# Weight tiles of the down projections: the low part made by an accumulating DMA in place of a VectorE subtraction

## The chip, the cores and the metric

The kernel runs on one core of a Trainium2 chip. The metric is device time in microseconds (us), from one launch to its end. The kernel before took 1015.24 us in the median of two runs (1014.68 and 1015.81).

## What is computed

The reference is a two-layer decoder trunk for 256 tokens of width 1024, in float32. Each layer is a feed-forward block, a token mixer with cross attention beside it, and a second feed-forward block:

```python
D_FF = 256 * ((8 * D_MODEL // 3 + 255) // 256)      # 2816

def swiglu(x, w_in, w_out):
    gate, up = jnp.split(x @ w_in, 2, axis=-1)
    return (jax.nn.silu(gate) * up) @ w_out
...
    for i in range(DEPTH):
        x = x + 0.5 * swiglu(rms_norm(x, ffn1_norm_g[i]), ffn1_w_in[i], ffn1_w_out[i])
...
        x = x + 0.5 * swiglu(rms_norm(x, ffn2_norm_g[i]), ffn2_w_in[i], ffn2_w_out[i])
```

The change concerns `@ w_out`, the down projection (2816 to 1024) of the four feed-forward blocks.

## The kernel before, in words

Activations are held transposed, 128 features on the partitions and 256 tokens along the row. Products are made on TensorE in a reduced float format (`F32R`), three for one: each operand is split into a high part (the value rounded to that format) and a low part (the value less its high part), and `mm3` (L226 to L230) issues high x high, high x low and low x high into one accumulator. The weights are split as they arrive, tile by tile, and each is used once.

A weight tile has 128 partitions x 4 chunks x 256 columns, 512 KB (2 chunks, 256 KB, for the last tile of each six in a down projection); a chunk of a partition is a run of 1 KB. `wtile` (L218) takes a raw buffer `wr` (5 of them, pool `wrp`), loads it by a DMA on SP's queue, and calls `split` (L208): ScalarE writes the high part `wh` by a copy (L213), and VectorE writes the low part `wl`, raw less high (L214). `wh` and `wl` have 8 buffers each. So at most 13 tiles can be under way ahead of TensorE: 8 split, and 5 raw.

Four feed-forward blocks run one after the other, with the two mixers between them (`program`, L1003). In `ffn` (L536) the up projection takes 44 tiles in eleven groups, then the down projection takes four column groups (`c2`) of 256 outputs; for each it walks the six tiles of `KG` (20 chunks in five tiles, then 2) and both halves `m` of the columns. At the end of each group VectorE scales the sum and adds it to the residual, and `Norm.put` prepares the next norm. The last group of the last block is written otherwise: it takes all six tiles first and then walks them twice (L552). 

TensorE and SP run in the order in which the program is written. The other engines' order is set by a scheduler, and each engine's queue is worked off in order. POOL (GpSimd) does little: a few small loads at the start and the powers of some norms (L253, L313, L406).

Of the kernel before, what the change touches and what calls it, by code (L numbers as in the profile page):

```python
# [10 lines left out]
F32 = mybir.dt.float32  # L11
F32R = mybir.dt.float32r
BF16 = mybir.dt.bfloat16
I32 = mybir.dt.int32
AF = mybir.ActivationFunctionType
ALU = mybir.AluOpType
# [3 lines left out]
P = 128  # L20
# [78 lines left out]
def tile_trunk(ctx: ExitStack, tc: tile.TileContext, a, out):  # L99
    nc = tc.nc  # L100
    seq = [0]

    def mk(pool, shape, dt, tag):
        seq[0] += 1
        return pool.tile(shape, dt, tag=tag, name=f"{tag}_{seq[0]}")

    def pool(name, bufs, **kw):
        return ctx.enter_context(tc.tile_pool(name=name, bufs=bufs, **kw))
# [11 lines left out]
    wrp = pool("wrp", 5)  # L120
    whp = pool("whp", 8)
    wlp = pool("wlp", 8)
# [10 lines left out]
    def act(*args, **kw):  # L133
        ins = nc.scalar.activation(*args, **kw)  # L134
        if args[2] not in (AF.Copy, AF.Square):
            tabled[0] = ins
# [6 lines left out]
    def unit(dt):  # L143
        return mk(up, [P, 2, T], dt, "u")

    def tmp():
        return mk(tp, [P, 2, T], F32, "t")
# [4 lines left out]
    def mo():  # L152
        return mk(pb8, [P, 512], F32, "bank")

    def halves(ps):
        return ps.rearrange("p (h t) -> p h t", h=2)
# [49 lines left out]
    last = [None]  # L206

    def split(src, shape):  # L208
        hi = mk(whp, shape, F32R, "wh")
        lo = mk(wlp, shape, F32R, "wl")  # L210
        n = shape[1] // pieces[0]
        for i in range(pieces[0]):
            last[0] = nc.scalar.copy(hi[:, i * n:(i + 1) * n], src[:, i * n:(i + 1) * n])  # L213
            tt(out=lo[:, i * n:(i + 1) * n], in0=src[:, i * n:(i + 1) * n],  # L214
               in1=hi[:, i * n:(i + 1) * n].bitcast(F32), op=ALU.subtract)
        return hi, lo

    def wtile(src, nk, ncol=256):  # L218
        raw = mk(wrp, [P, nk, ncol], F32, "wr")
        nc.sync.dma_start(raw, src)  # L220
        return split(raw, [P, nk, ncol])

    def wcols(w, c0, kh):
        return wtile(w.rearrange("(k p) f -> p k f", p=P)[:, kh * 4:(kh + 1) * 4, c0:c0 + 256], 4)

    def mm3(ps, wh, wl, xh, xl, start, stop):  # L226
        nc.tensor.matmul(ps, wh, xh, start=start, stop=False, skip_group_check=True)  # L227
        nc.tensor.matmul(ps, wh, xl, start=False, stop=False, skip_group_check=True)  # L228
        nc.tensor.matmul(ps, wl, xh, start=False, stop=stop, skip_group_check=True)  # L229
        wv.now += 0.328  # L230
# [24 lines left out]
    def pair(x):  # L255
        return x.unsqueeze(1).to_broadcast([P, 2, T])
# [170 lines left out]
    def memory():  # L427
# [8 lines left out]
        for c2 in range(4):  # L436
            nc.sync.dma_start(memT[c2], a["memT"][:, 2 * c2:2 * c2 + 2])
            hi, lo = unit(F32R), unit(F32R)
            for m in range(2):
                split_gain(memT[c2][:, m], g(G_MEM + 2 * c2 + m), hi[:, m], lo[:, m])  # L440
            mh.append(hi)
            ml.append(lo)
            if c2 == 0:
                v = wkv.rearrange("(k p) f -> p k f", p=P)
                wfirst.append([wtile(v[:, k:k + 2, 0:256], 2) for k in (0, 2)])
            if c2 == 2:
                wfirst.append(wcols(wkv, 0, 1))
# [50 lines left out]
    def ffn_in(x, w_in, hh, hl, mid=None):  # L498

        def hidden(ps):  # L500
            t = tmp()
            for m in range(2):
                tt(out=t[:, m], in0=ps[m][:, :T], in1=x.rb, op=ALU.mult)  # L503
            act(t, t, AF.Silu)
            for m in range(2):
                tt(out=t[:, m], in0=t[:, m], in1=ps[m][:, T:], op=ALU.mult)  # L506
            hi, lo = unit(F32R), unit(F32R)
            split_plain(t, hi, lo)
            hh.append(hi)
            hl.append(lo)  # L510

        waiting = []
        for gi in range(11):
            ps = [mo(), mo()]
            for kh in range(2):
                for part in range(2):
                    wh, wl = wcols(w_in, part * FF + gi * 256, kh)
                    for m in range(2):
                        for k in range(4):
                            kc = kh * 4 + k  # L520
                            mm3(ps[m][:, part * T:(part + 1) * T],
                                wh[:, k, m * P:(m + 1) * P], wl[:, k, m * P:(m + 1) * P],
                                x.xh[kc // 2][:, kc % 2], x.xl[kc // 2][:, kc % 2],
                                start=kc == 0 and part == 0, stop=kc == 7)
                        yield
            waiting.append(ps)
            if gi == 0 and not x.done:
                continue
            yield x.ready
            for ps in waiting:  # L530
                hidden(ps)
            waiting.clear()
            if mid is not None and gi == 5:
                wv.spawn(mid())

    def ffn(x, w_in, w_out, nxt=None, mid=None):  # L536

        pieces[0] = 1
        hh, hl = [], []
        yield from ffn_in(x, w_in, hh, hl, mid)  # L540
        w = w_out.rearrange("(k p) f -> p k f", p=P)

        def products(ps, m, kg, wt, start):
            ms = slice(m * P, (m + 1) * P)
            for k in range(kg[1]):
                kc = kg[0] + k
                mm3(ps, wt[0][:, k, ms], wt[1][:, k, ms], hh[kc // 2][:, kc % 2], hl[kc // 2][:, kc % 2],
                    start=kc == 0 and start, stop=kc == 21)

        for c2 in range(4):  # L550
            wts = [(kg, w[:, kg[0]:kg[0] + kg[1], c2 * 256:(c2 + 1) * 256]) for kg in KG]
            if nxt is None and c2 == 3:  # L552
                wts = [(kg, wtile(src, kg[1])) for kg, src in wts]
                y = tmp()
                for m in range(2):
                    ps = mo()[:, :T]
                    for kg, wt in wts:
                        products(ps, m, kg, wt, True)
                        yield
                    tt(out=y[:, m], in0=ps, in1=x.hrb, op=ALU.mult)  # L560
                    tt(out=y[:, m], in0=y[:, m], in1=x.xT[c2][:, m], op=ALU.add)
                    nc.scalar.dma_start(out[:, 2 * c2 + m], y[:, m])
                return
            ps = mo()
            for kg, src in wts:
                wt = wtile(src, kg[1])
                for m in range(2):
                    products(ps[:, m * T:(m + 1) * T], m, kg, wt, m == 0)
                    yield
            t = tmp()  # L570
            tt(out=t, in0=halves(ps), in1=pair(x.hrb), op=ALU.mult)
            xn = unit(F32)
            tt(out=xn, in0=t, in1=x.xT[c2], op=ALU.add)
            if nxt is None:
                nc.scalar.dma_start(out[:, 2 * c2:2 * c2 + 2], xn)
            else:
                nxt.put(xn)
        wv.spawn(nxt.chain(), LAT['norm'])
# [424 lines left out]
    def program():  # L1003
        yield from memory()
        x1, x2, x3 = Norm(G_MIX, half=False, cols=True), Norm(G_F2), Norm(G_F1 + 8)
        x4, x5 = Norm(G_MIX + 8, rows=False), Norm(G_F2 + 8)
        yield from ffn(x0, a["ffn1_w_in"][0], a["ffn1_w_out"][0], x1, late_constants)
        yield from mixer_a(x1, x2)
        yield from ffn(x2, a["ffn2_w_in"][0], a["ffn2_w_out"][0], x3)
        yield from ffn(x3, a["ffn1_w_in"][1], a["ffn1_w_out"][1], x4, rope_tables)  # L1010
        yield from mixer_b(x4, x5)
        yield from ffn(x5, a["ffn2_w_in"][1], a["ffn2_w_out"][1])
# [41 lines left out]
```

## Time and profile before

| what | value |
|---|---|
| median of two runs | 1015.24 us |
| span of the profiled execution, first to last instruction | 1011.9 us |
| mean granted TensorE clock | 0.997 |
| busy: PE, DVE, ACT, POOL | 98%, 67%, 52%, 3% |
| DMA traffic | 182.71 MB, 181 GB/s over the span |
| weight tiles split | 347 pairs of L213 and L214 |

The profiled execution's own time beside its span is not listed; the median of the runs lies 3.3 us above the span. The page gives busy times, shares in 40 slices, DMA queues, and the chain of work that ended last, followed back from the last instruction. PE is TensorE's matmuls and PEld its weight loads, DVE is VectorE, ACT is ScalarE, SP is the queue that issues the weights' loads, and a queue's number in the DMA part (q1, q0) stands for SP's and POOL's issues. In a row of a group `out<-in` are the program's tiles, with the mean of one and the idle time ahead of it behind the bar. In a row of the waits stand the waiting instruction, what released it, total us, times, and the longest.

### The profile page before, as it was taken

How to read it: one execution, taken by the hardware profiler on the slowest of the kernel's cores; microseconds unless marked ns; L12 is line 12 of the kernel's file. 1: busy time of each engine (PE TensorE's matmuls, PEld its weight loads, DVE VectorE, ACT ScalarE, POOL GpSimd, SP SyncE). 2: the span in 40 equal slices, each digit the busy share in tenths (PEclk: the TensorE clock that was granted, in tenths of full speed). 3: DMA queues.
4: the chain of work that ended last, by engine and by line, in shares of the span. 5: the costliest groups of instructions: out<-in, count | busy, mean ns of one | idle time of the engine just before them, and what ended most of it. 6: DMA issues, size and time to landing. Idle time of an engine off the chain costs nothing.

```text
span 1011.9 us, 20587 instructions
## 1 busy us (share of the span) xinstructions
PE 996.4 (98%) x8560; PEld 978.2 (97%) x8560; DVE 673.3 (67%) x1116; ACT 524.0 (52%) x771; POOL 28.5 (3%) x27
## 2 busy tenths in 40 slices
PE   8899999999999999999999999999999999999998
PEld 7899999999999999999999999999987899999998
DVE  6876665668756786666568666656787768666551
ACT  7755444456566564454445444544557665454440
POOL 1100000000100000000000000000121000000000
PEclk9999999999999999999999999999999999999999
DMA  9676666667644566665666666566632247665650
GB/s 310 209 247 189 193 190 180 190 187 204 184 131 138 178 191 199 193 191 178 192 206 201 200 189 192 178 194 199 189 115 81 87 137 222 199 190 183 189 171 22
DMA packets 173205, 182.71 MB, mean 181 GB/s; under 512 B 7124, under 2 KB 168328, under 8 KB 173112
## 3 DMA queue, kind: packets, MB, share of 16 engines
q1 hardware_dynamic: 171872, 179.60, 58.3%
q10 hardware_dynamic: 1016, 1.58, 0.5%
q8 instruction: 67, 1.10, 0.5%
q0 software_dynamic: 224, 0.22, 0.2%
q14 instruction: 26, 0.21, 0.1%
HBM read 180.32 MB, written 1.05 MB: 179 GB/s over the span
## 4 chain that ended last, share of the span: by engine, by line
PE 92%; DVE 4%; ACT 1%; POOL 1%; DMA 1%; issue 0%; SPq 0%; POOLq 0%; ACTq 0%; DVEq 0%
PE bank L227 29%; PE bank L228 29%; PE bank L229 29%; PE bank L233 2%; DVE wl L214 1%; PE bank L238 1%; POOL col L406 1%; ACT u L134 1%; DMA wr<-in_mem_w_kv_dram 1%; PE bank L988 1%; DVE col L401 0%; DVE u L410 0%; DVE u L973 0%; DVE col L957 0%; ACT wh L213 0%
## 5 line engine op out<-in xcount | busy, mean ns | idle before, releaser
L214 DVE TENSOR_TENSOR wl<-wr,wh 128x1024 fp32r<-128x1024 f32 (+1 forms) x347 | 414.7, 1196 | 267.0 <-ACT wh L213 266.2
L213 ACT CAST wh<-wr 128x1024 fp32r<-128x1024 f32 (+1 forms) x347 | 356.9, 1031 | 391.8 <-PE bank L228 367.4
L227 PE MATMUL bank<-xh,wh 128*128 128x256 f32 x1544 | 427.8, 277 | 0.0
L228 PE MATMUL bank<-xl,wh 128*128 128x256 f32 x1544 | 426.4, 276 | 0.0
L229 PE MATMUL bank<-xh,wl 128*128 128x256 f32 x1544 | 426.4, 276 | 0.0
L227 PEld LDWEIGHTS bank<-xh,wh 128*128 128x128 f32 x1544 | 290.0, 188 | 0.1
L228 PEld LDWEIGHTS bank<-xl,wh 128*128 128x128 f32 x1544 | 289.8, 188 | 0.1
L229 PEld LDWEIGHTS bank<-xh,wl 128*128 128x128 f32 x1544 | 289.8, 188 | 0.0
L227 PE MATMUL bank<-u,wh 128*128 128x256 f32 x896 | 249.3, 278 | 0.0
L228 PE MATMUL bank<-u,wh 128*128 128x256 f32 x896 | 247.6, 276 | 0.0
L229 PE MATMUL bank<-u,wl 128*128 128x256 f32 x896 | 247.6, 276 | 0.0
L227 PEld LDWEIGHTS bank<-u,wh 128*128 128x128 f32 x896 | 168.2, 188 | 1.9 <-issue 1.7
L228 PEld LDWEIGHTS bank<-u,wh 128*128 128x128 f32 x896 | 168.3, 188 | 0.1
L229 PEld LDWEIGHTS bank<-u,wl 128*128 128x128 f32 x896 | 168.3, 188 | 0.0
L227 PE MATMUL bank<-wh,xh 128*128 128x256 f32 x208 | 60.3, 290 | 0.0
L228 PE MATMUL bank<-wl,xh 128*128 128x256 f32 x208 | 58.7, 282 | 0.0
L229 PE MATMUL bank<-wh,xl 128*128 128x256 f32 x208 | 58.5, 281 | 0.0
L503 DVE TENSOR_TENSOR t<-bank,rb 128x256 f32<-128x256 f32 x88 | 36.3, 420 | 6.7 <-PE bank L229 6.7
L227 PEld LDWEIGHTS bank<-wh,xh 128*128 128x128 f32 x208 | 39.8, 191 | 0.5 <-issue 0.3
L228 PEld LDWEIGHTS bank<-wl,xh 128*128 128x128 f32 x208 | 39.8, 191 | 0.1
L229 PEld LDWEIGHTS bank<-wh,xl 128*128 128x128 f32 x208 | 39.8, 191 | 0.0
L506 DVE TENSOR_TENSOR t<-t,bank 128x256 f32<-128x256 f32 x88 | 32.7, 413 | 0.0
(182 smaller groups left out, 671.0 us busy)
## 6 DMA issues: line engine op xcount, KB each, us to landing
wr<-in_ffn_w_in_dram SPq DMA_DIRECT2D x176, 512.0 KB, 4.3
wr<-in_ffn_w_out_dram SPq DMA_DIRECT2D x80, 512.0 KB, 3.7
wr<-in_a_w_in_dram SPq DMA_DIRECT2D x28, 512.0 KB, 3.7
wr<-in_b_w_in_dram SPq DMA_DIRECT2D x14, 512.0 KB, 4.6
wr<-in_a_w_out_dram SPq DMA_DIRECT2D x12, 512.0 KB, 3.4
wr<-in_b_w_out_dram SPq DMA_DIRECT2D x12, 512.0 KB, 3.4
wr<-in_ffn_w_out_dram SPq DMA_DIRECT2D x16, 256.0 KB, 2.9
wr<-in_mem_w_kv_dram SPq DMA_DIRECT2D x7, 512.0 KB, 7.8
```

What stands on the lines that cost most here:

```text
L134: ins = nc.scalar.activation(*args, **kw)
L213: last[0] = nc.scalar.copy(hi[:, i * n:(i + 1) * n], src[:, i * n:(i + 1) * n])
L214: tt(out=lo[:, i * n:(i + 1) * n], in0=src[:, i * n:(i + 1) * n], in1=hi[:, i * n:(i + 1) * n].bitcast(F32), op=ALU.subtract)
L227: nc.tensor.matmul(ps, wh, xh, start=start, stop=False, skip_group_check=True)
L228: nc.tensor.matmul(ps, wh, xl, start=False, stop=False, skip_group_check=True)
L229: nc.tensor.matmul(ps, wl, xh, start=False, stop=stop, skip_group_check=True)
L233: nc.tensor.matmul(ps, lhsT, rhs, start=start, stop=stop, skip_group_check=True)
L238: nc.tensor.transpose(ps, src, ident[:k, :k])
L406: nc.gpsimd.tensor_tensor(out=u[:, 8:8 + 2 * n], in0=u[:, 0:2 * n], in1=mhalf[:, 0:2 * n], op=ALU.pow)
L503: tt(out=t[:, m], in0=ps[m][:, :T], in1=x.rb, op=ALU.mult)
L506: tt(out=t[:, m], in0=t[:, m], in1=ps[m][:, T:], op=ALU.mult)
L988: nc.tensor.matmul(o[es[e], cs], vr[:, i, js], pTs[e][:, src], start=i == 0, stop=i == 1, skip_group_check=True)
```

## The change

A second function makes weight tiles, and the down projections call it, except the last column group of the last block: 24 tiles in each of the first three blocks and 18 in the last, 90 in all.

```diff
+    def wtile_dma(src, nk):
+
+        raw = mk(wrp, [P, nk, 256], F32, "wr")
+        hi, lo = mk(whp, [P, nk, 256], F32R, "wh"), mk(wlp, [P, nk, 256], F32R, "wl")
+        nc.sync.dma_start(raw, src)
+        act(lo, raw, AF.Copy, scale=-1.0)
+        nc.gpsimd.dma_start(lo, src, accum_op=ALU.add)
+        last[0] = nc.scalar.copy(hi, raw)
+        return hi, lo
...
             ps = mo()
             for kg, src in wts:
-                wt = wtile(src, kg[1])
+                wt = wtile_dma(src, kg[1])
                 for m in range(2):
```

ScalarE writes the negative of the rounded weights into the low tile, and a DMA issued on POOL's queue reads the same weights from DRAM once more and adds them onto it, so that the low tile holds the weight less its rounded value. The raw load on SP's queue and the copy to the high tile stay. VectorE has no part in these tiles any more. TensorE's third product of a triple, the first that reads the low tile, waits for the DMA where it waited for VectorE.

The order of TensorE's and SP's instructions is the same as before but for line numbers, which are 10 higher below the new function. On ScalarE, at the start of the first down projection, there stood before (`t` and `u` belong to the up projection's groups, `wh` and `wl` to weight tiles):

```order
L213 CAST wh_1987<-wr_1985 128x1024
L134 ACTIVATE t_1751<-t_1751 128x512
L213 CAST wh_2028<-wr_2026 128x1024
L247 CAST u_1757<-t_1751 128x512
L213 CAST wh_2058<-wr_2056 128x1024
L213 CAST wh_2088<-wr_2086 128x1024
```

And now:

```order
L213 CAST wh_1987<-wr_1985 128x1024
L134 ACTIVATE t_1751<-t_1751 128x512
L230 CAST wh_2027<-wr_2026 128x1024
L257 CAST u_1757<-t_1751 128x512
L134 ACTIVATE wl_2028<-wr_2026 128x1024
L230 CAST wh_2058<-wr_2057 128x1024
L134 ACTIVATE wl_2059<-wr_2057 128x1024
L230 CAST wh_2089<-wr_2088 128x1024
```

Each tile has a second instruction on ScalarE, behind the high part's; the up projection's instructions keep their places between them.

On POOL, from the powers of the memory's keys to those of the first mixer, there stood before (`col` are the norms' columns):

```order
L406 TENSOR_TENSOR col_418<-col_418,mhalf_116 128x4
L185 DMA u_110<-in_mask_dram 128x384
L406 TENSOR_TENSOR col_3160<-col_3160,mhalf_116 128x4
L406 TENSOR_TENSOR col_3233<-col_3233,mhalf_116 128x4
L253 TENSOR_TENSOR col_3798<-col_3809,mhalf_116 128x2
```

Now the 24 accumulating DMAs of the first block stand between them, of which these are the first three:

```order
L416 TENSOR_TENSOR col_418<-col_418,mhalf_116 128x4
L185 DMA u_110<-in_mask_dram 128x384
L229 DMA wl_2028<-in_ffn_w_out_dram 128x4x256
L229 DMA wl_2059<-in_ffn_w_out_dram 128x4x256
L229 DMA wl_2090<-in_ffn_w_out_dram 128x4x256
```

and these the last two, with the mixer's powers behind them:

```order
L229 DMA wl_2715<-in_ffn_w_out_dram 128x4x256
L229 DMA wl_2746<-in_ffn_w_out_dram 128x2x256
L416 TENSOR_TENSOR col_3184<-col_3184,mhalf_116 128x4
L416 TENSOR_TENSOR col_3257<-col_3257,mhalf_116 128x4
L263 TENSOR_TENSOR col_3822<-col_3833,mhalf_116 128x2
```

No power stands between the DMAs of one block.

## Prediction

> **What bounds the kernel now.** I read the page's shares and slices first, then the chain that ended last, then the waits, and at last the one stage that the change touches. From the page:
>
> ```profile
> span 1011.9 us, 20587 instructions
> PE 996.4 (98%) x8560; PEld 978.2 (97%) x8560; DVE 673.3 (67%) x1116; ACT 524.0 (52%) x771; POOL 28.5 (3%) x27
> PE   8899999999999999999999999999999999999998
> DMA  9676666667644566665666666566632247665650
> PE 92%; DVE 4%; ACT 1%; POOL 1%; DMA 1%; issue 0%; SPq 0%; POOLq 0%; ACTq 0%; DVEq 0%
> ```
>
> TensorE is busy in every slice and carries 92% of the chain. VectorE, which the change relieves, carries 4%. So a saving on VectorE is worth only what TensorE waits for it. All such waits on a low part, in the whole run and then in the first down projection (window 160 to 220; columns: total us, times, longest):
>
> ```profile
> PEld bank L228 <- DVE wl L214: 3.4, 2, 2.3
> PE bank L228 <- DVE wl L214: 3.0, 2, 2.1
> ...
> ACT wh L213 <- PE bank L228: 30.2, 21, 2.1
> DVE wl L214 <- ACT wh L213: 24.1, 19, 2.5
> ```
>
> The first two rows are the whole price of late low parts, and they lie elsewhere: within the down projection TensorE is not among the waiting engines. There ScalarE waits for TensorE (a place in the ring of eight), and VectorE for ScalarE. TensorE sets the pace. Its pace and the other engines' room, from the tile's rows and from three windows (us, busy of PE, PEld, DVE, ACT, POOL, clock, DMA share, GB/s):
>
> ```profile
> L227 PE MATMUL bank<-u,wh x176: 276/276/276, 160.3 to 219.8; 128*128 128x256 f32 x176
> L229 PE MATMUL bank<-u,wl x176: 276/276/276, 160.5 to 220.0; 128*128 128x256 f32 x176
> ...
> 160.00:220.00 60.00, 60.00 (x532) 60.00 (x531) 35.52 (x43) 30.32 (x36) 0.00 (x0) 1.00 0.66 183
> 143.00:219.00 76.00, 76.00 (x673) 76.00 (x672) 45.60 (x55) 36.34 (x44) 0.00 (x0) 1.00 0.65 185
> 12.00:20.00 8.00, 7.13 (x58) 6.93 (x59) 7.78 (x11) 6.76 (x10) 0.00 (x0) 1.00 1.07 392
> ```
>
> A down projection has 24 tiles, 20 of four chunks and 4 of two: 22 full ones. It runs from 160.3 to 220.1, so 59.8 / 22 = 2.72 us of TensorE for a full tile (512 KB). The DMA share is already 0.65 there.
>
> **The change, part by part.**
>
> Removed: 90 subtractions on VectorE (three FFNs with 24 tiles, the last with 18; 82.5 full ones).
>
> ```profile
> L214 DVE TENSOR_TENSOR wl<-wr,wh 128x1024 fp32r<-128x1024 f32 (+1 forms) x347 | 414.7, 1196 | 267.0 <-ACT wh L213 266.2
> L213 ACT CAST wh<-wr 128x1024 fp32r<-128x1024 f32 (+1 forms) x347 | 356.9, 1031 | 391.8 <-PE bank L228 367.4
> ```
>
> That is about 90 x 1.2 = 108 us of VectorE time, all beside TensorE: worth 0, by the waits above.
>
> Added on ScalarE: a second pass over each tile, the negative copy. I price it like the cast, 1.05 us for a full tile: 22 x 1.05 = 23 us in a window in which ScalarE is busy 30.3 of 60. It fits (53 of 60), and the places in the ring give it a lead, below. Worth 0. If the pass cost twice the cast, ScalarE would need 77 of 60 us, but nothing speaks for that: the same engine, one input and one output of the same size.
>
> Added on POOL: 90 DMA issues. The nearest rows are POOL's own issues:
>
> ```profile
> 2.14 0.59 POOL L187 DMA_DIRECT2D sink<-in_b_sinks_dram  x1
> 2.72 0.73 POOL L188 DMA_DIRECT2D posi<-in_positions_dram  x1
> 36.66 0.61 POOL L185 DMA_DIRECT2D u<-in_mask_dram  x1
> ```
>
> The sink and the mask have 128 pieces, the positions 256; the new DMA has 512. 128 more pieces cost 0.14 us, so I estimate 0.59 + 3 x 0.14 = 1.0 us, under the 2.72 us at hand; the other end, four times 0.6 and twice for two operands, is 4.8 us (a rival, below). Each issue waits for ScalarE's negative copy. Behind it on POOL stand only further accumulations and, after the 24th, the mixer's powers, whose inputs come later. Nobody waits for those in the stage.
>
> Added to the transfers: per tile, an accumulation that reads the same 512 KB from DRAM a second time, reads the 512 KB of negatives back from the low tile, and writes 512 KB. This is the term that counts. Latency first. SP's loads and ScalarE's casts around the first down projection:
>
> ```profile
> 130.05 61.61 SPq L220 DMA_DIRECT2D wr<-in_ffn_w_out_dram  x24
> 143.65 48.01 SPq L220 DMA_DIRECT2D wr<-in_ffn_w_out_dram  x19
> 193.02 17.68 SPq L220 DMA_DIRECT2D wr<-in_a_w_in_dram  x8
> 215.77 7.54 SPq L220 DMA_DIRECT2D wr<-in_a_w_in_dram  x4
> ...
> 141.31 1.05 ACT L213 CAST wh<-wr 128x1024 fp32r<-128x1024 f32 x1 [1.14 <-PE bank L228]
> 154.91 0.62 ACT L213 CAST wh<-wr 128x512 fp32r<-128x512 f32 x1 [1.15 <-PE bank L228]
> ...
> wr<-in_ffn_w_out_dram SPq DMA_DIRECT2D x80, 512.0 KB, 3.7
> u<-in_mask_dram POOLq DMA_DIRECT2D x1, 192.0 KB, 4.5
> ```
>
> The 512-column cast at 154.91 is the sixth tile's, so the first tile's is five casts earlier, at 141.31. TensorE reads that tile from 160.3 on. After two passes on ScalarE the first accumulation can start at 143.4: 17 us of lead against 4 to 5 us of landing. A single accumulation is hidden. A sustained stream is another matter.
>
> Throughput: from 143.4 to 218.7, when TensorE starts the 24th tile (220.1 less half of 2.72), are 75.3 us. I take off 2.3 for the last landing (3.7 less the transfer itself, 1.4), which leaves 73.0 us of DMA time. How fast the DMA engines go when nothing holds them back, the window 12 to 20 shows: 392 GB/s at a share of 1.07, or 366 at 1.0, which is 524,288 / 366,000 = 1.43 us for a plain full tile. (The other end is the stage's own ratio, 185 / 0.65 = 285 GB/s, 1.84 us. I take 1.43, since queues that are behind look like the start.) In those 73 us SP's loads go on: 19 tiles of this stage (17 full ones) and about 10 of the next, 27 x 1.43 = 38.6 us. For 22 accumulations 34.4 us are left: 1.56 us each is the break-even, 1.09 times a plain tile.
>
> What an accumulation costs, no row of the trace shows. Low end: as a plain tile, 1.43 us, hidden; a gain is excluded, since TensorE waits for nothing here. High end: the packets that POOL's queue has moved so far.
>
> ```profile
> q1 hardware_dynamic: 171872, 179.60, 58.3%
> q0 software_dynamic: 224, 0.22, 0.2%
> ```
>
> 58.3% of 16 x 1011.9 us over 171,872 packets are 55 ns; 0.2% over 224 are 145 ns. 512 pieces on 16 engines at 145 ns are 4.64 us. I take twice a plain tile, 2.86 us, because two operands of 512 KB have to be read for each tile: it is nearest to the plain loads, which are pieces of the same 1 KB, while the 224 packets are mostly tiny or of another size. The Trainium skill (Collectives: The Full Stack, "The bandwidth ceiling: the fold count and why AG ≠ RS ≠ AR") says that adding in a DMA costs no cycles of its own but needs two source reads, and gives a copy-to-reduce ratio of 1.93. No row here shows it; by it an accumulation would take 2.76 us by estimate and the sum would end at 1106 us.
>
> The sum, for each of the first three FFNs: 22 x 2.86 = 62.9, less 34.4, is 28.5 us late. Once TensorE has caught up with the ring it waits for the low part in each tile. The lead is regained in the next up projection, at 2.72 - 1.43 us a tile, so each stage starts afresh. For the last FFN:
>
> ```profile
> 917.87 61.61 SPq L220 DMA_DIRECT2D wr<-in_ffn_w_out_dram  x24
> ```
>
> shifted by 787.8 from the first: accumulations from 931.2, and the 18th tile (16.5 full ones) needed at 948.1 + 16 x 2.72 = 991.6. That is 60.4 - 2.3 = 58.1 us, 24.3 of them for 17 plain tiles; 33.8 are left for 16.5 x 2.86 = 47.2: 13.4 late. Together 3 x 28.5 + 13.4 = 98.9, and 1011.9 + 98.9 = 1110.8 for the span. The runs' median, 1015.24, lies 3.3 above the profiled span, and I add that: 1114.
>
> **The rivals.**
>
> Hidden anyway (not slower): the read of the negatives costs nothing beside the DRAM read, and an accumulation passes as a plain tile. Place: the 34.4 us. Then 22 x 1.43 = 31.5 fit, and the time is 1015. It decides up to 1.56 us per accumulation. For it speaks the share of 0.65; against it, that it has 9% to spare and two operands to carry. The Trainium skill (DMA: Bandwidth & Descriptors, Specifications) limits a core's DRAM traffic to about 358 GB/s. If only DRAM bytes counted, that would be 1.46 us a tile by estimate, 49 x 1.46 = 71.5 of 73 us, and 1015 as well; but the trace's 392 GB/s is above that limit, so the limit is not what binds here.
>
> The accumulation itself is slow: the read, add and write of each 1 KB piece do not overlap as plain pieces do. At 4.64 us: 3 x (102.1 - 34.4) + (76.6 - 33.8) = 246 us, so 1261. It decides from about 2.5 times a plain tile. For it: the 145 ns of POOL's queue; against: the mixture of those packets.
>
> POOL becomes the bound: writing out the pieces takes it longer than TensorE needs. From 73.0 / 22 = 3.3 us per full tile on; at 4.8 us 3 x (105.6 - 73) + (79.2 - 58.1) = 119 us, so 1134. Against it: 0.73 us for 256 pieces.
>
> **How the numbers follow.** Twice a plain tile (1.5 to 2.5 times): 0.42, with 1114 and a range of its own from 1055 to 1173 by the same sum. Hidden: 0.18. Slow accumulation: 0.28. POOL: 0.10. A gain, from VectorE's lighter load in places that the waits don't show: 0.02. A measurement of this kernel tells about 2% from no change, 20 us; hidden falls within that, all others are above it. So faster 0.02, same 0.18, slower 0.80. The range goes from 1014 (hidden) to 1300, above the 145 ns case and above the 1.84 us case (twice 1.84 gives 3 x 57.7 + 33.9 = 207, or 1222); it leaves out a slower add still.
>
> **What would show it.** Queue q0 moves 82.5 x 0.524 = 43 MB more. The DMA share goes to about 1.0 in the four down projections and stays as it was in the up projections. TensorE waits for the accumulations at the third product of the triples (L239 of the changed kernel), some 100 us in all, and the first tiles of each stage show no wait. POOL's issues take about 1 us each. ScalarE's negative copies take about 1.05 us. I am wrong about the mechanism if TensorE waits in the stage while the DMA share stays near 0.65 (then POOL, or the latency of the pieces, is the limit), and wrong about the size if an accumulation is not near 2.9 us.

## The result, and the profile after

The changed kernel takes 1119.39 us in the median of two runs (1119.28 to 1119.50), against 1015.24 before: 1.103 times as long, with a 95% interval of 1.101 to 1.106. The profiled execution's span is 1117.7 us, 105.8 more than before. The page of the changed kernel, its shares, slices, chain and DMA queues:

```profile
span 1117.7 us, 20772 instructions
PE 1021.0 (91%) x8560; PEld 991.0 (89%) x8560; DVE 575.9 (52%) x1026; ACT 602.4 (54%) x861; POOL 142.3 (13%) x117
PE   8899997679999999998779999967899999999867
DMA  8776699997634576689998666999932347668992
PE 40%; issue 15%; DMA 12%; POOL 5%; DVE 3%; ACT 2%; POOLq 0%; ACTq 0%; DVEq 0%
q1 hardware_dynamic: 171872, 179.60, 53.3%
q0 software_dynamic: 43904, 43.48, 24.3%
```

TensorE's slices have four dips, and in the same slices, but for the very last, the DMA row stands at 9: the four down projections. TensorE has fallen from 92% to 40% of the chain. VectorE's 97 us of saved work have bought nothing. The new traffic is on q0, 43.48 MB.

The waits of the changed kernel that concern these tiles (total us, times, longest):

```profile
PEld bank L239 <- DMA wl<-in_ffn_w_out_dram: 89.7, 53, 3.5
PE bank L239 <- DMA wl<-in_ffn_w_out_dram: 79.0, 51, 3.3
ACT wh L230 <- DMA wr<-in_ffn_w_out_dram: 56.2, 32, 3.3
```

The groups of the two new instructions, POOL's issue and ScalarE's negative copy, from its page:

```profile
L229 POOL DMA_DIRECT2D wl<-in_ffn_w_out_dram x90 | 113.6, 1264 | 700.5 <-ACT wl L134 696.8
L134 ACT ACTIVATE wl<-wr 128x1024 fp32r<-128x1024 f32 x90 | 88.4, 982 | 28.7 <-DMA wr<-in_ffn_w_out_dram 14.2
```

And the time from issue to landing of the two streams (the last number, us):

```profile
wr<-in_ffn_w_out_dram SPq DMA_DIRECT2D x80, 512.0 KB, 16.2
wl<-in_ffn_w_out_dram POOLq DMA_DIRECT2D x75, 512.0 KB, 19.4
```

PEld and PE are two views of one wait, so they are not added. TensorE waits for the accumulating DMA and, in this stage, for nothing else of note. The raw loads, which landed after 3.7 us before, now take 16.2, as they would if both streams stood in one line. ScalarE waits for raw tiles, where it waited for TensorE before. POOL is idle for 700 us, waiting for ScalarE, most of it between the stages.

How long each down projection lasts shows in the first and last start of its low-part products (L239; us):

```profile
L239 PE MATMUL bank<-u,wl x176: 276/276/386, 160.6 to 246.5; 128*128 128x256 f32 x176
L239 PE MATMUL bank<-u,wl x176: 276/276/520, 501.8 to 589.0; 128*128 128x256 f32 x176
L239 PE MATMUL bank<-u,wl x176: 276/276/415, 710.2 to 797.2; 128*128 128x256 f32 x176
L239 PE MATMUL bank<-u,wl x176: 276/276/415, 1034.1 to 1113.6; 128*128 128x256 f32 x176
```

Five windows of the changed kernel, one ahead of the first stage, one in its middle, and three of 5 us at the end of the last (busy of PE, PEld, DVE, ACT, POOL, then clock, DMA share, GB/s):

```profile
143.00:160.00 17.00, 17.00 (x152) 17.00 (x152) 3.41 (x7) 13.14 (x16) 7.63 (x6) 1.00 0.99 205
180.00:240.00 60.00, 40.58 (x328) 38.22 (x329) 9.57 (x15) 28.77 (x36) 15.12 (x12) 1.00 1.18 238
1085.00:1090.00 5.00, 3.41 (x26) 3.21 (x27) 2.18 (x3) 1.05 (x1) 0.00 (x0) 1.00 1.17 238
1090.00:1095.00 5.00, 2.92 (x26) 2.72 (x25) 1.23 (x1) 1.05 (x1) 0.00 (x0) 1.00 1.07 264
1095.00:1100.00 5.00, 5.00 (x46) 5.00 (x46) 2.02 (x3) 1.57 (x2) 0.00 (x0) 1.00 0.08 20
```

Before, each lasted 59.5 us (160.5 to 220.0). Now they last 85.9, 87.2, 87.0 and 79.5: late by 26.4, 27.7, 27.5 and 20.0, together 101.6 of the 105.8 us. The other 4.2 lie between the stages. The windows show the lead being used up: up to 160 TensorE is never idle, and from 180 on it works 40.6 of 60 us, while the DMA engines move 238 GB/s. At the end of the last stage the engines go on at that rate or above it up to 1095, and do almost nothing after.

The granted clock does not explain the lateness: it shows as 1.00 in every 10 us from 160 to 250, where the first stage is late by 26.4 us, and where it dips, as to 0.83 in 770 to 780, the stage is late by about as much (27.5).

TensorE's last wait in the first stage and in the last, and ScalarE's casts of the fourth and the fifth tile of the stage behind the first:

```profile
242.59 0.39 PE L239 MATMUL bank<-u,wl 128*128 128x256 f32 x1 [1.45 <-DMA wl<-in_ffn_w_out_dram]
1094.77 0.38 PE L239 MATMUL bank<-u,wl 128*128 128x256 f32 x1 [2.08 <-DMA wl<-in_ffn_w_out_dram]
241.23 1.04 ACT L213 CAST wh<-wr 128x1024 fp32r<-128x1024 f32 x1 [2.00 <-DMA wr<-in_a_w_in_dram]
245.40 1.05 ACT L213 CAST wh<-wr 128x1024 fp32r<-128x1024 f32 x1 [3.12 <-PE bank L239]
```

A full tile has eight low-part products. From 242.59 on 12 of them are left in the first stage, a tile and a half; from 1094.77 on 56 in the last, seven tiles, of which five and a half are the last group's. So the last wait is for the last full accumulated tile, the 23rd and the 17th, and not for the half tile behind it, whose accumulation POOL issued right after (the two from 223.67 and from 1073.95 on). And when the first stage's last wait ended, four tiles of the next stage had landed.

### The profile page after: what moved, and what is told of

The parts are those of the page before. It is cut to its first block, busy times and chain, and to the rows that moved or that the text cites. A ratio compares the mean times of both kernels' runs of the same rounds, so it can differ in the third digit from the quotient of the medians.

```text
span 1117.7 us, 20772 instructions
## 1 busy us (share of the span) xinstructions
PE 1021.0 (91%) x8560; PEld 991.0 (89%) x8560; DVE 575.9 (52%) x1026; ACT 602.4 (54%) x861; POOL 142.3 (13%) x117
## 3 DMA queue, kind: packets, MB, share of 16 engines
q0 software_dynamic: 43904, 43.48, 24.3%
HBM read 223.58 MB, written 1.05 MB: 201 GB/s over the span
## 4 chain that ended last, share of the span: by engine, by line
PE 40%; issue 15%; DMA 12%; POOL 5%; DVE 3%; ACT 2%; POOLq 0%; ACTq 0%; DVEq 0%
PE bank L237 12%; PE bank L239 12%; PE bank L238 12%; DMA wr<-in_ffn_w_out_dram 5%; DMA wl<-in_ffn_w_out_dram 4%; POOL wl L229 4%; DMA wr<-in_b_w_in_dram 3%; PE bank L243 2%; DVE wl L214 1%; PE bank L248 1%; ACT u L134 1%; POOL col L416 1%; ACT wh L213 1%; PE bank L998 1%; ACT wl L134 0%
## 5 line engine op out<-in xcount | busy, mean ns | idle before, releaser
L214 DVE TENSOR_TENSOR wl<-wr,wh 128x1024 fp32r<-128x1024 f32 (+1 forms) x257 | 312.3, 1217 | 266.7 <-ACT wh L213 263.0
L239 PE MATMUL bank<-xh,wl 128*128 128x256 f32 x1544 | 426.6, 276 | 0.0
L213 ACT CAST wh<-wr 128x1024 fp32r<-128x1024 f32 (+1 forms) x257 | 268.0, 1047 | 292.1 <-PE bank L238 204.3
L239 PE MATMUL bank<-u,wl 128*128 128x256 f32 x896 | 256.9, 287 | 79.1 <-DMA wl<-in_ffn_w_out_dram 79.0
L239 PEld LDWEIGHTS bank<-xh,wl 128*128 128x128 f32 x1544 | 289.8, 188 | 0.0
L237 PE MATMUL bank<-u,wh 128*128 128x256 f32 x896 | 252.8, 282 | 0.0
L238 PE MATMUL bank<-u,wh 128*128 128x256 f32 x896 | 251.0, 280 | 0.0
L239 PEld LDWEIGHTS bank<-u,wl 128*128 128x128 f32 x896 | 171.1, 191 | 89.8 <-DMA wl<-in_ffn_w_out_dram 89.7
L229 POOL DMA_DIRECT2D wl<-in_ffn_w_out_dram x90 | 113.6, 1264 | 700.5 <-ACT wl L134 696.8
L237 PEld LDWEIGHTS bank<-u,wh 128*128 128x128 f32 x896 | 171.2, 191 | 1.9 <-issue 1.7
L238 PEld LDWEIGHTS bank<-u,wh 128*128 128x128 f32 x896 | 171.4, 191 | 0.1
L230 ACT CAST wh<-wr 128x1024 fp32r<-128x1024 f32 x90 | 87.8, 975 | 97.4 <-DMA wr<-in_ffn_w_out_dram 56.2
L134 ACT ACTIVATE wl<-wr 128x1024 fp32r<-128x1024 f32 x90 | 88.4, 982 | 28.7 <-DMA wr<-in_ffn_w_out_dram 14.2
L239 PE MATMUL bank<-wh,xl 128*128 128x256 f32 x208 | 58.6, 282 | 0.5 <-DVE xl L253 0.5
L253 DVE SCALAR_TENSOR_TENSOR xl<-u,gcol,xh 128x256 fp32r<-128x256 f32 x48 | 21.0, 477 | 59.8 <-ACT xh L134 59.8
## 6 DMA issues: line engine op xcount, KB each, us to landing
wr<-in_ffn_w_out_dram SPq DMA_DIRECT2D x80, 512.0 KB, 16.2
wr<-in_ffn_w_out_dram SPq DMA_DIRECT2D x16, 256.0 KB, 16.1
```

The lines of the kernel that those rows point to most:

```text
L229: nc.gpsimd.dma_start(lo, src, accum_op=ALU.add)
L230: last[0] = nc.scalar.copy(hi, raw)
L253: nc.vector.scalar_tensor_tensor(out=lo, in0=src, scalar=gc, in1=hi.bitcast(F32), op0=ALU.mult, op1=ALU.subtract)
```

## The experiments

The theory was the prediction's: in a down projection the DMA engines have too little time, since an accumulation costs them two reads, and the lateness is what does not fit into the room. Rivals: POOL's queue is slow whatever it moves; the doubled DRAM traffic; the new waits, POOL's issues and ScalarE's pass; a fixed price per piece; the adder.

**The price by itself (e1_units).** A program with nothing but streams of transfers, each stream waiting for the end of the one before it:

```diff
+    def pool_plain_1k(i):
+        t, src = one_k(i)
+        nc.gpsimd.dma_start(t.bitcast(F32), src)
...
+    def pool_add_1k(i):
+        t, src = one_k(i)
+        nc.gpsimd.dma_start(t, src, accum_op=ALU.add)
...
+    def pool_add_sbuf(i):
+        nc.gpsimd.dma_start(bufs[i % 8], rows[i % 5], accum_op=ALU.add)
+
+    def both(i):
+        nc.sync.dma_start(rows[i % 5], tiles[i])
+        pool_add_1k(i)
```

> Leaves out the whole computation: eight streams one after the other, 16 transfers of 512 KB each, at most eight in flight. Theory (an accumulation costs the DMA engines two reads): plain loads, from SP or from POOL, in 1 KB or 4 KB pieces, near 1.4 us each; the same load with the cast to the reduced format near 1.4; accumulations near 2.9 in 1 KB pieces, not much less in 4 KB pieces, and near 2.9 with the source in the core's memory as well; the two streams together 4.4 us a pair. Rival one (POOL's queue is slow whatever it moves): the plain load from POOL takes near 2.9 too. Rival two (a fixed price per piece of an accumulation): 4 KB pieces take an accumulation to under 2 us. Rival three (DRAM bytes): the accumulation from the core's memory is well below 2.9.

Eight transfers are in flight, and each further issue waits for a buffer to come free, so the distance between POOL's issues is the price of one. The first and last such issue of six streams, from the program's timeline (start us): plain (L147), plain with the cast (L151), accumulation in 1 KB pieces (L155), in 4 KB pieces (L159), from the core's memory (L162), and beside SP's loads (L155 once more):

```profile
71.53 0.75 POOL L147 DMA_DIRECT2D big<-in_ffn_w_out_dram  x1 [0.81 <-DMA big<-in_ffn_w_out_dram]
79.07 0.75 POOL L147 DMA_DIRECT2D big<-in_ffn_w_out_dram  x1 [0.76 <-DMA big<-in_ffn_w_out_dram]
101.71 0.74 POOL L151 DMA_DIRECT2D big<-in_ffn_w_out_dram  x1 [0.78 <-DMA big<-in_ffn_w_out_dram]
106.24 0.74 POOL L151 DMA_DIRECT2D big<-in_ffn_w_out_dram  x1 [0.79 <-DMA big<-in_ffn_w_out_dram]
135.23 1.27 POOL L155 DMA_DIRECT2D big<-in_ffn_w_out_dram  x1 [0.98 <-DMA big<-in_ffn_w_out_dram]
145.93 1.29 POOL L155 DMA_DIRECT2D big<-in_ffn_w_out_dram  x1 [1.39 <-DMA big<-in_ffn_w_out_dram]
178.67 0.85 POOL L159 DMA_DIRECT2D big<-in_ffn_w_out_dram  x1 [1.65 <-DMA big<-in_ffn_w_out_dram]
191.24 0.84 POOL L159 DMA_DIRECT2D big<-in_ffn_w_out_dram  x1 [1.44 <-DMA big<-in_ffn_w_out_dram]
222.49 0.85 POOL L162 DMA_DIRECT2D big<-r  x1 [1.53 <-DMA big<-r]
235.83 0.84 POOL L162 DMA_DIRECT2D big<-r  x1 [1.81 <-DMA big<-r]
276.92 1.27 POOL L155 DMA_DIRECT2D big<-in_ffn_w_out_dram  x1 [2.78 <-DMA big<-in_ffn_w_out_dram]
298.90 1.27 POOL L155 DMA_DIRECT2D big<-in_ffn_w_out_dram  x1 [3.11 <-DMA big<-in_ffn_w_out_dram]
```

With five, three, four, five, five and five steps between them, a 512 KB transfer takes 1.51 us plain, 1.51 with the cast, 2.68 as an accumulation, 2.51 in 4 KB pieces, 2.67 from the core's own memory, and a raw load and an accumulation together 4.40. SP's plain loads alone, from the same program's windows in 1 KB and in 4 KB pieces (busy of DVE and POOL, clock, DMA share, GB/s), move a tile in 524,288 / 349,000 = 1.50 and 1.31 us:

```profile
16.00:34.00 18.00, 1.54 (x6) 0.00 (x0) 1.00 1.10 349
42.00:58.00 16.00, 0.00 (x0) 0.00 (x0) 1.00 1.00 399
```

So POOL's queue is not slow by itself, and DRAM is not the price: a source in the core's memory costs 2.67. The number of pieces matters little to an accumulation (2.68 in 512 pieces, 2.51 in 128), more to SP's plain loads (1.50 and 1.31). The pair is what the kernel does, and 4.40 less the prediction's 1.43 for a plain tile is 2.97 for the accumulation; with the 1.50 measured here it is 2.90. As a rate the pair moves 2 x 524,288 bytes in 4.40 us, 238 GB/s, the rate of the changed kernel's window from 180 to 240.

**What the second cost is (e7_adder).** The same program with source and destination in the core's memory, in four forms, of which these are three:

```diff
+    def add_f32(i):
+        nc.gpsimd.dma_start(bufs[i % 8].bitcast(F32), rows[i % 5], accum_op=ALU.add)
+
+    def add_bf16(i):
+        nc.gpsimd.dma_start(bufs[i % 8].bitcast(BF16), rows[i % 5].bitcast(BF16), accum_op=ALU.add)
+
+    def plain_f32(i):
+        nc.gpsimd.dma_start(bufs[i % 8].bitcast(F32), rows[i % 5])
```

> Leaves out the whole computation: four streams of 16 transfers of 512 KB from POOL, source and destination in the core's memory: plain float32, accumulation into the reduced format, into float32, and as bfloat16 (the same bytes, twice the elements). Theory (bytes read): plain 1.4 to 1.5 us each, each accumulation 2.66, the bfloat16 one too. Rival one (the adder's elements): 5.3 for bfloat16. Rival two (the format's cast): the float32 accumulation near 1.5.

First and last issue of the steady part, plain (L175), accumulating in float32 (L169) and in bfloat16 (L172):

```profile
23.77 0.53 POOL L175 DMA_DIRECT2D big<-r  x1 [0.99 <-DMA big<-r]
26.55 0.53 POOL L175 DMA_DIRECT2D big<-r  x1 [0.84 <-DMA big<-r]
96.45 0.85 POOL L169 DMA_DIRECT2D big<-r  x1 [1.84 <-DMA big<-r]
107.09 0.85 POOL L169 DMA_DIRECT2D big<-r  x1 [1.79 <-DMA big<-r]
141.82 0.85 POOL L172 DMA_DIRECT2D big<-r  x1 [1.81 <-DMA big<-r]
152.47 0.85 POOL L172 DMA_DIRECT2D big<-r  x1 [1.82 <-DMA big<-r]
```

Plain 2.78 / 2 = 1.39 us; float32 10.64 / 4 = 2.66; bfloat16, with twice the elements in the same bytes, 10.65 / 4 = 2.66. The accumulation into the reduced format takes 2.65 by the same reading. The price follows bytes, not additions or formats, at 1.91 times a plain copy. That fits a second read; no run separates the read from other work per byte. The Trainium skill's 1.93 for a reduction (Collectives: The Full Stack, "The bandwidth ceiling: the fold count and why AG ≠ RS ≠ AR") agrees with this 1.91. In the kernel's own form, 1 KB pieces from DRAM, the ratio of the streams by themselves is 2.68 / 1.51 = 1.77.

**The same kernel without the add (e2_no_add).**

```diff
-        nc.gpsimd.dma_start(lo, src, accum_op=ALU.add)
+        nc.gpsimd.dma_start(lo, src)
```

> The changed kernel with the add taken out of its DMA: the same 90 transfers of the same weights from POOL overwrite the negatives, so the low part is the weight itself. POOL's issues, ScalarE's second pass, the waits and the DRAM bytes stay. Theory: 22 x 1.43 = 31.5 us of a stage's 34.4, so 1015 to 1030. Rival (the second DRAM read, POOL's queue or the added waits cost it): as the changed kernel, near 1119.

It takes 1014.50 us, 0.9997 of before (0.9988 to 1.0007; in each experiment the kernel before was run again beside it): the whole loss is gone, with the same 43.48 MB on q0 and the same waits in the program. POOL's issue is shorter without the add, 0.74 us in the median; the next experiment keeps its length.

**With the add cut to an eighth of the bytes (e3_narrow):**

```diff
-        nc.gpsimd.dma_start(lo, src, accum_op=ALU.add)
+        nc.gpsimd.dma_start(lo[:, :, :32], src[:, :, :32], accum_op=ALU.add)
```

> The changed kernel with the accumulation cut to the first 32 of 256 columns of each chunk, so the other columns' low part is the negative alone. 512 pieces and all issues, passes and waits stay; the bytes fall to an eighth. Theory (bytes through the DMA engines): 1015 to 1025. Rival (POOL's issue, ScalarE's pass or the latency): near 1119. Rival (price per piece): 1080 or more.

1014.73 us, 1.0004 (0.9995 to 1.0014). POOL's issues have the same length as in the changed kernel, 1277 ns in the median of both, and TensorE does not wait for them. The window of the first down projection in e2_no_add:

```profile
143.00:219.00 76.00, 76.00 (x673) 76.00 (x672) 19.88 (x31) 56.45 (x68) 17.68 (x24) 1.00 1.17 329
```

The same window in e3_narrow:

```profile
143.00:219.00 76.00, 76.00 (x673) 76.00 (x672) 20.35 (x31) 56.46 (x68) 30.34 (x24) 1.00 0.96 204
```

And the length of e3_narrow's issues on POOL (ns: shortest, median, longest):

```profile
L229 POOL DMA_DIRECT2D wl<-in_ffn_w_out_dram x90: 1183/1277/1850, 144.2 to 975.7; - x90
```

So neither the DRAM bytes (329 GB/s in e2_no_add, 238 in the changed kernel), nor POOL, nor ScalarE's pass, nor the wait for a DMA costs anything here. What is left is the accumulation's load on the DMA engines.

**Fewer accumulated tiles (e4_half, e5_two_thirds, e8_all_but_third).** The other tiles are split as before:

```diff
-                wt = wtile_dma(src, kg[1])
+                wt = (wtile_dma if (kg[0] // 4) % 2 == 0 else wtile)(src, kg[1])    # e4_half: 12 of 22
+                wt = (wtile_dma if (kg[0] // 4) % 3 != 2 else wtile)(src, kg[1])    # e5_two_thirds: 16 of 22
+                wt = (wtile_dma if kg[0] // 4 != 2 else wtile)(src, kg[1])          # e8_all_but_third: 18 of 22
```

> Only the first, third and fifth tile of each column group take the accumulating DMA, 12 of 22 full ones in a stage; the others are split as before. Theory: 12 x 2.97 = 35.6 against 34.4 us, and 9 x 2.97 = 26.7 against 33.8 in the last FFN: 1015 to 1025, so more than half of the DMAs for nothing. Rival (each accumulated tile costs its share, a latency or a wait per tile): 104 x 12/22 = 57 more, near 1072.

> The accumulating DMA for four of the six tiles of each column group (all but the third and the half tile), 16 of 22 full ones in a stage. Theory with the price of the streams just measured (4.40 us a pair, less 1.43, is 2.97 us): 16 x 2.97 = 47.5 against 34.4, three times 13.1, and 12 x 2.97 = 35.6 against 33.8 in the last FFN: 41 us more, 1055. Rival (a cost per accumulated tile): 104 x 16/22 = 76 more, 1090. Nothing more at all (1015) would say that the limit is not the room in the stage.

> The accumulating DMA for five of the six tiles of each column group (all but the third), 18 of 22 full ones in a stage. Theory with the prediction's room: 18 x 2.97 = 53.5 against 34.4, three times 19.1, and 13.5 x 2.97 = 40.1 against 33.8: 64 more, 1078. Theory with the room as read from the stages of the two-thirds kernel (late by 9.5, 8.4, 7.7 and 4.8 us with 16 tiles, by 26.4, 27.7, 27.5 and 20.0 with 22): about 3.1 us a tile more, so 15 us in each of three stages and 10 in the last, 55 more, 1069. Rival (a cost per accumulated tile): 104 x 18/22 = 85, 1099.

Measured: 1014.52 us (1.000, 0.999 to 1.001), 1053.68 (1.038, 1.036 to 1.041) and 1071.3 (1.055, 1.054 to 1.057). Twelve tiles in 22 are free, and from 16 on the time climbs: a threshold between them, not a price per tile. But the sum for two thirds came out right partly by accident. The first and the last stage of e5_two_thirds:

```profile
L239 PE MATMUL bank<-u,wl x176: 276/276/394, 161.5 to 230.5; 128*128 128x256 f32 x176
L239 PE MATMUL bank<-u,wl x176: 276/276/386, 985.1 to 1049.4; 128*128 128x256 f32 x176
```

Its matmuls in 40 us of the third up projection (the number behind PE's busy time):

```profile
580.00:620.00 40.00, 40.00 (x342) 40.00 (x342) 24.35 (x32) 18.45 (x22) 0.00 (x0) 1.00 0.60 186
```

And in 40 us of the same up projection in the kernel before:

```profile
560.00:600.00 40.00, 40.00 (x356) 40.00 (x355) 25.03 (x34) 19.39 (x22) 0.00 (x0) 1.00 0.61 190
```

The four stages are late by 9.5, 8.4, 7.7 and 4.8, together 30.4 us, where the sum said 41; the other 11.3 of the span's 41.7 lie outside the stages, 6.5 of them in that up projection, which lasted 126.7 us (552.8 to 679.5) in place of 120.2, and where the matmuls came every 117 ns (40 us / 342) in place of 112 without a wait. A second profile asked whether that was a passing state:

> The two-thirds kernel once more, for a second profile: in the first, TensorE's matmuls in one up projection came every 119 ns in place of 113, without a wait, which made 6.5 of its 41.7 us. If that is a passing state of that execution, this profile is some 6 us shorter, near 1047 by its span, with the same late stages; if the kernel brings it about, it is there again.

It was there again (342 matmuls in 40 us, span 1050.9, median 1055.09 us of two runs), so this kernel brings it about; why is open. For e8_all_but_third the matmuls kept their pace (356 in 40 us), and the stages were late by 14.6, 16.4, 14.1 and 6.7: 51.8 us against the 55 expected from the stages of its neighbours.

Its first and last stage:

```profile
L239 PE MATMUL bank<-u,wl x176: 276/276/387, 162.5 to 236.6; 128*128 128x256 f32 x176
L239 PE MATMUL bank<-u,wl x176: 276/276/418, 999.5 to 1065.7; 128*128 128x256 f32 x176
```

**The lead (e6_ring6_after, and e6b_ring6_before as its control).**

```diff
-    whp = pool("whp", 8)
-    wlp = pool("wlp", 8)
+    whp = pool("whp", 6)
+    wlp = pool("wlp", 6)
```

> The changed kernel with 6 in place of 8 high and low buffers. Theory (the room is the time between the first negative copy and the last tile's use): two places fewer start the accumulations 2 x 2.72 = 5.4 us later and keep two plain loads of 1.43 out of the room, so 2.6 us more per stage, some 10 in all: 1129. Rival (the lead does not matter, the stream alone sets the time): 1119.

> The kernel before with 6 in place of 8 high and low buffers, as the control: 1015 to 1020 by every theory, since the split tiles lead TensorE by more than the two passes take.

The control takes 1014.41 us (1.000, 0.999 to 1.001): before, two places were spare. The changed kernel takes 1136.21, 1.120 times before (1.117 to 1.123), 17 us more than with eight. The lead matters, but by more than the 10 us expected. The first stage of e6_ring6_after:

```profile
L239 PE MATMUL bank<-u,wl x176: 276/276/443, 161.1 to 252.6; 128*128 128x256 f32 x176
```

SP's loads for the stage behind it, in the same kernel:

```profile
215.84 31.65 SPq L220 DMA_DIRECT2D wr<-in_a_w_in_dram  x8
```

And in the changed kernel:

```profile
210.09 31.27 SPq L220 DMA_DIRECT2D wr<-in_a_w_in_dram  x8
```

The stage lasts 91.5 us, 5.6 more, near the two places' 2 x 2.72 = 5.4, and its first accumulation is issued at 149.63 in place of 144.27. The loads that I had thought would stay out of the room did not: eight of them are issued beside the accumulations in both kernels. The four stages together last 21.7 us longer than with eight places; the rest of the run is 3.3 shorter, and the runs leave open why.

## Why the prediction was right, point by point

- VectorE's subtractions worth nothing: right. All three kernels that drop some or all of them and are not late end within 0.1% of before.
- ScalarE's second pass, 1.05 us predicted: the median is 1.054, and e2_no_add and e3_narrow hide it.
- POOL's issue, 1.0 us predicted from 128 and 256 pieces: 1.28 measured, hidden as said. The rise was right for an accumulation, (1.27 - 0.85) / 3 = 0.14 us per 128 pieces in e1_units; the start was not, 0.85 at 128 pieces in place of 0.59. The plain DMA with 512 pieces takes 0.75.
- Latency hidden by the lead: right. TensorE is busy through 143 to 160 and begins the stage at 160.6, as before.
- The price, 2.86 us by two plain tiles: 2.90 to 2.97 in the pair, 2.68 alone. Right in size; its reason, the second read, fits the price by bytes but was not shown apart from other work per byte.
- The room, 34.4 us: a little more, and made up otherwise. The sum counted ten loads of the next stage in it. Eight are issued beside the accumulations, since SP too is held back; with 25 plain tiles the room is 73.0 - 25 x 1.43 = 37.2, and 22 x 2.97 - 37.2 = 28.1 us against the 26.4, 27.7 and 27.5 measured; for 18 tiles 16.3 against 15.0 on average, for 16 tiles 10.3 against 8.5, for 12 nothing. But not all eight had landed by the last wait, and the sum set its deadline a tile late, at the half tile in place of the full tile ahead of it. The first stage's trace shows four loads landed, others under way, a deadline 2.7 us earlier and a lead of 16.1 us in place of 16.9. With 21 to 22 plain tiles the room is then 73.0 - 2.7 - 0.8 less 30.0 to 31.5, that is 39.5 to 38.0 us, and the lateness 65.3 less that, 25.8 to 27.3 against 26.4. So the price was too low and the room too small, and the two nearly cancelled: the 28.5 us of the sum came this close partly by luck.
- The last stage, 13.4 us predicted: 20.0. This term was mis-sized. Here SP's last load was issued at 1083.4, and the DMA engines were all but done by 1095, when the last wait ended: all 17 plain tiles of the sum went beside the accumulations, and no smaller count makes up for the late deadline. With 2.97, the deadline at the 17th tile and the lead of 16.1 us it is 49.0 - (58.1 - 2.7 - 0.8 - 24.3) = 18.7 us; 1.3 stay open.
- The end of the sum, 3.3 us between span and time: in the changed kernel's profiled run it is 1119.50 - 1117.7 = 1.8. Together the first three stages came out 3.9 us under the sum, the last 6.6 over it, and 4.2 lie between the stages, where the sum had nothing: 98.9 predicted, 105.8 measured. That the total is this near is in part such cancelling.
- The rivals: hidden anyway would have needed 1.56 us per accumulation, or the 12 tiles of e4_half; a slow accumulation of 4.64 us and a POOL of 4.8 us are both excluded by e1_units.
- What the profile was to show: q0 with 43 MB, right; TensorE waiting at L239, right, and in no stage in its first 15 us; some 100 us of such waits, too many: 79.0, while the same 8560 matmuls count as busy 24.6 us longer; the DMA share at about 1.0, wrong: it is 1.18, and in e2_no_add it is 1.17 with no lateness at all.

## What to carry to other kernels

Before giving work to a DMA, add up what the DMA engines must do in the stage where it will run, with an accumulation counted as two transfers, and compare it with that stage's time, up to the last tile that is waited for: a relief on an engine that nobody waits for pays for nothing. A stage that overruns is late only by what exceeds its lead, so half of such a change may be free and the rest dear; try the fraction before the whole. And the rate of a saturated pair of streams, measured by itself (238 GB/s in e1_units), tells whether the stage runs at that limit: 238 GB/s was also what the down projection moved.

## What the runs showed of the hardware that I had not expected

- The DMA share does not say how much room is left: 1.17 with 329 GB/s and nobody waiting (e2_no_add), 1.18 with 238 GB/s and TensorE waiting for a third of the time (the changed kernel, 180 to 240).
- An accumulating DMA costs POOL more to issue than a plain one of the same 512 pieces: 1.27 us against 0.75; with 128 pieces of 4 KB it is 0.85 against 0.53 (the latter within the core's memory).
- The matmuls' pace can change without a wait: 117 ns in place of 112 through one up projection of the two-thirds kernel, twice, with the granted clock shown as 1.00. The cause is open.
